# Fifty-eight gate and up chunks with the weights stationary and 256 tokens moving

## The chip, the core and the metric

The kernel runs on one core of one Trainium2 chip. The metric is the device time of one launch in microseconds (us), the median of three runs. PE is TensorE's matmul, PEld its weight load (the operand that stands in the array is loaded once for every matmul instruction), DVE is VectorE, ACT ScalarE, POOL GpSimd, SP SyncE.

## What is computed

Two blocks of two layers each over 256 tokens of width 1024, in float32. There are six feed-forward networks (FFN) of hidden width 2816, one after each mixer and in the first block one ahead of it too; the mixers (a short convolution, differential attention, retention, stick-breaking attention) are not touched by the change.

```python
def swiglu(x, w_gu, w_down):
    gate, up = jnp.split(x @ w_gu, 2, axis=-1)
    return (jax.nn.silu(gate) * up) @ w_down

h = h + 0.5 * rmsnorm(swiglu(rmsnorm(h, g[0]), ffn_w_gu[l, 0], ffn_w_down[l, 0]), g[1])
...
x = x + swiglu_2(rms_norm(x, ffn_norm[i]), ffn_w_in[i], ffn_w_out[i])
```

## The kernel before

The 256 tokens are two halves of 128. A product is kept exact to float32 by splitting each operand into a high and a low part of type fp32r and adding three products: high by high, high by low, low by high.

**Weights.** `plan` lists the weights as 279 units of 128 x 2048 numbers (1 MB each), in the order of use. `Weights.load` brings a unit to a `raw` tile, `split` makes `whi` on ACT (L162) and `wlo` on DVE (L163), each in two pieces of 128 x 1024 ahead of other work (`high_priority`). `pump` splits as long as one of five slots is free. On the host, `layout` orders the numbers of each row of 512 so that a read which takes columns 0, 256, 1, 257, ... (`columns`, "p (r a) -> p a r") gives the true order. Every weight moves in that alternating order.

**Tokens.** `T_gain` transposes a half of h and writes it with the norm's gain as `xT` (high and low): hidden index on the partitions, 128 tokens in a row. It is the operand that stands in PE. The norm's factor `rstd` is per token, that is per partition of the product, and is applied when the product is read.

**An FFN** (`ffn`) has 11 chunks of 256 hidden columns. For a chunk, `gu` runs for each half and each of two units four steps of `mm_col` with three matmuls (`mm3`, L259 to L261): tokens stand, 512 weight columns (256 gate, 256 up) move, and 128 tokens x 512 columns gather in one of two PSUM banks `mm`. Then ACT applies SiLU to the gate (L397), DVE multiplies with up (L399), which gives `hid`, tokens on partitions. The second product needs it the other way round, so `tr` transposes it on PE, two 128 x 128 blocks a half (L408, `tr_h`), and `split_plain` writes `hT` high (ACT, L310) and low (DVE, L311). `dn` then multiplies `hT` of two chunks earlier with a down unit into `acc` (`mm_row`, L282, L285, L288).

**Order.** A chunk in the steady state is 48 matmuls of `gu`, 24 of `dn` and 4 transposes. Four FFNs (f01, f11, f20, f21) have `skew`: their chunks 0 and 1 run by halves as `heads`, between the steps of the previous stage's end. f00 and f10 run all chunks in `body`. Engines run in the order that a scheduler gives at build time.

Of the kernel before, what the change touches and what calls it, by code (L numbers as in the profile page):

```python
# [11 lines left out]
F32 = mybir.dt.float32  # L12
F32R = mybir.dt.float32r
AF = mybir.ActivationFunctionType
ALU = mybir.AluOpType
# [3 lines left out]
P = 128  # L19
D = 1024  # L20
KD = D // P
FF = 2816
NCH = FF // 256
# [6 lines left out]
SLACK = 30  # L30
PIECES = 2


def plan():

    units = []

    def cols(key, w, idx, *segs):
        for j in range(2):
            units.append(((key, j), w, idx, 4 * j, segs))

    def row(key, j, w, idx):
        units.append(((key, j), w, idx, 2 * j, ((0, D),)))

    def ffn(tag, w_gu, w_dn, idx):  # L50
        for c in range(NCH):
            cols((tag, "gu", c), w_gu, idx, (c * 256, 256), (FF + c * 256, 256))
            if 2 <= c < NCH - 1:
                row((tag, "dn"), c - 2, w_dn, idx)
        for c in range(NCH - 3, NCH):
            row((tag, "dn"), c, w_dn, idx)

    def chunks(tag, w, which):
        for c in which:
            cols((tag, c), w, (0,), (c * 512, 512))  # L60

    def rows(tag, w, which):
        for j in which:
            row(tag, j, w, (0,))

    ffn("f00", "ffn_w_gu", "ffn_w_down", (0, 0))
    for c in range(4):
        cols(("cz", c), "conv_w_in", (0,), (D + c * 256, 256), (2 * D + c * 256, 256))
    chunks("cb", "conv_w_in", range(2))
    rows("co", "conv_w_out", range(4))  # L70
    ffn("f01", "ffn_w_gu", "ffn_w_down", (0, 1))
    for c in range(2):
        cols(("kv", c), "w_kv", (), (c * 512, 512))
    ffn("f10", "ffn_w_gu", "ffn_w_down", (1, 0))
    chunks("q", "attn_w_q", range(2))
    for c in range(2, 4):
        cols(("kv", c), "w_kv", (), (c * 512, 512))
    rows("ao", "attn_w_o", range(4))
    ffn("f11", "ffn_w_gu", "ffn_w_down", (1, 1))
    chunks("ri", "ret_w_in_2", range(11))  # L80
    rows("ro", "ret_w_o_2", range(2))
    chunks("ri", "ret_w_in_2", [11])
    rows("ro", "ret_w_o_2", range(2, 8))
    ffn("f20", "ffn_w_in_2", "ffn_w_out_2", (0,))
    chunks("si", "sb_w_in_2", [0, 1, 2, 4, 3, 5])
    rows("so", "sb_w_o_2", range(4))
    ffn("f21", "ffn_w_in_2", "ffn_w_out_2", (1,))
    return units


def layout(inputs):

    a = {name: np.asarray(v) for name, v in inputs.items()}
    units = plan()
    w = np.empty((len(units), P, 2048), np.float32)
    for i, (_, name, idx, k0, segs) in enumerate(units):
        nk = 2048 // sum(n for _, n in segs)
        rows = a[name][idx][k0 * P : (k0 + nk) * P].reshape(nk, P, -1).transpose(1, 0, 2)
        np.concatenate([rows[:, :, c : c + n] for c, n in segs], axis=2, out=w[i].reshape(P, nk, -1))
        w[i] = w[i].reshape(P, 4, 256, 2).transpose(0, 1, 3, 2).reshape(P, 2048)  # L100
    gains = [a["norm_g"], a["mix_norm_2"], a["ffn_norm_2"], a["ret_out_norm_2"], a["conv_k"], a["kv_norm_g"]]
    gains += [a["sb_q_norm_2"]] * 2 + [a["sb_k_norm_2"]] * 2 + [a["attn_subln_g"]]
    return {
        "x": a["x"],
        "x_t": np.ascontiguousarray(a["x"][0].reshape(2, P, KD, P).transpose(0, 3, 2, 1)),
        "w": w,
        "gains": np.ascontiguousarray(np.concatenate([g.ravel() for g in gains]).reshape(-1, P).T),
        "norm_g": a["norm_g"],
        "attn_lambda": a["attn_lambda"],
        **constants(),  # L110
    }
# [74 lines left out]
def tile_two_models(ctx: ExitStack, tc: tile.TileContext, a: dict):  # L186
# [6 lines left out]
    const = pool("const", 1)  # L193
    raw_pool = pool("raw", RAW)
    part_pool = pool("part", SLOTS)
    xt_pool = pool("xt", 1)
    k8 = pool("k8", 1)
    k4 = pool("k4", 4)
# [23 lines left out]
    gains = const.tile([P, NG], F32, tag="gains", name="gains")  # L222
    h = [const.tile([P, D], F32, tag=f"h{i}", name=f"h{i}") for i in range(2)]

    def g_cols(first, n):
        return gains[:, first : first + n]

# [20 lines left out]
    def new_mm():  # L248
        return ps_mm.tile([P, 512], F32, tag="mm", name="mm")

    def new_tr(name):
        return ps_tr.tile([P, 512], F32, tag="tr", name=name)
# [21 lines left out]
    def mm_row(acc, xT, kts, key, j, first, end, last):  # L274
# [14 lines left out]
        if last:  # L289
            W.done((key, j))  # L290

    def new_xT(half, place=None):
        if place is not None:
            t = big(place, [P, 2, KD, P], F32R, f"xk{half}")
        else:
            t = xt_pool.tile([P, 2, KD, P], F32R, tag=f"xT{half}", name=f"xT{half}")
        return t[:, 0], t[:, 1]

    def split_gain(tr, gcols, hi, lo):

# [8 lines left out]
    def split_plain(tr, hi, lo):  # L309
        S.copy(hi, tr)  # L310
        V.tensor_tensor(lo, tr, hi.bitcast(F32), ALU.subtract)  # L311
# [11 lines left out]
    def rms_of(half):  # L323
        ms, r = small(tag="ms"), small(tag=f"rstd{half}")
        S.activation(junk(D), h[half], AF.Square, scale=1 / 32, accum_out=ms)
        power(r, ms, EPS)
        return r


    def add_plain(half, acc):  # L330
# [54 lines left out]
    def ffn(tag, xT, rstd, skew=True, first=None, last_stage=False):  # L385
# [4 lines left out]
        def gu(c, half, j, last=True):  # L390
# [3 lines left out]
            if j == 1:  # L394
# [4 lines left out]
                V.scalar_tensor_tensor(t, ps[:, 256:512], rstd[half], sg, ALU.mult, ALU.mult)  # L399
                hid[c, half] = t  # L400

        def tr(c, half):
            if c not in hT:
                hT[c] = k4.tile([P, 2, 2, 2, P], F32R, tag="k4", name=f"hT{c}")
            t = new_tr("tr_h")
            src = hid.pop((c, half))
            for k in range(2):
                T.transpose(t[:, k * P : k * P + P], src[:, k * P : k * P + P], ident)  # L408
            split_plain(t[:, 0:256].rearrange("p (k t) -> p k t", k=2), hT[c][:, half, 0], hT[c][:, half, 1])
# [19 lines left out]

        def body():  # L430
            nonlocal first
            if not skew:
                for c in range(2):
                    for j in range(2):
                        for half in range(2):
                            gu(c, half, j, last=half == 1)
                            if first is not None:
                                first()
                                first = None
                        W.pump()  # L440
                    if c == 1:
                        for half in range(2):
                            tr(0, half)
            for c in range(2, NCH):
                for j in range(2):
                    for half in range(2):
                        gu(c, half, j, last=half == 1)
                        if c == 2 and j == 0:
                            tr(1, half)
                    W.pump()  # L450
                if c < NCH - 1:
                    for half in range(2):
                        dn(c - 2, half, last=half == 1)
                        tr(c, half)
                    W.pump()

        def tail_step(c, half):
            def run():
                dn(c, half, last=half == 1)
                if half == 0 and c == NCH - 3:  # L460
                    tr(NCH - 1, 0)
                if half == 0 and c == NCH - 2:
                    tr(NCH - 1, 1)

            return run

# [176 lines left out]
    def attention(xT, rstd, xk, rstd_k, kT):  # L643
# [67 lines left out]
        def s3(g, half):  # L711
            nh, n, s, sums = st.pop((g, half))
            sv = sums.rearrange("p (h c) -> p h c", c=2)
            if half not in r0s:
                r0s[half] = small(8, tag=f"r0{half}")
                if half == 0:
                    asb[half] = k4.tile([P, 8, n], F32, tag="k4", name="aA")
                else:
                    asb[half] = xt_pool.tile([P, 8, n], F32, tag="xT1", name="aB")
            hs = slice(g * nh, g * nh + nh)  # L720
            rec = small(8, tag="rec")[:, 0 : 2 * nh]
            V.reciprocal(rec, sums)
            rv = rec.rearrange("p (h c) -> p h c", c=2)
            cf = small(4, tag="cf")[:, 0:nh]
            V.scalar_tensor_tensor(cf, rv[:, :, 1], nlam, sv[:, :, 0], ALU.mult, ALU.mult)
            V.tensor_copy(r0s[half][:, hs], rv[:, :, 0])
            for i in range(nh):
                V.scalar_tensor_tensor(
                    asb[half][:, g * nh + i], s[:, i, 1], cf[:, i : i + 1], s[:, i, 0], ALU.mult, ALU.add
                )  # L730
# [290 lines left out]
    def stick(xT, rstd):  # L1021
# [56 lines left out]
        def l1(i):  # L1078
# [14 lines left out]
            if i < 6:  # L1093
                l, sp = (k4.tile([P, D], F32, tag="k4", name=n)[:, 0 : 6 * P] for n in ("l", "sp"))
            else:
                t = xt_pool.tile([P, 2, 6 * P], F32, tag=f"xT{i - 6}", name=f"l{i}")
                l, sp = t[:, 0], t[:, 1]
            l, sp = (t.rearrange("p (e t) -> p e t", e=2) for t in (l, sp))
            if i == 6:
# [269 lines left out]
```

## Time and profile before

| | us |
|---|---|
| median of 3 runs | 1613.62 (1613.02 to 1614.09) |
| the profiled execution | 1613.5 |
| its span on the core | 1611.7 |
| PE busy | 1580.7, 98% of the span |
| PEld busy (beside PE) | 1360.0, 84% |
| DVE busy | 968.6, 60% |
| ACT busy | 863.2, 54% |

Some 2 us lie around the span. The granted TensorE clock is 0.999 of full speed over the whole span, which is the level of 2.4 GHz. A matmul's busy time is its way through the array and overlaps the next one's; what a matmul costs in a stream is the distance from one start to the next, read from a timeline or from the chain that ended last.

### The profile page before, as it was taken

Reading aid. Unit: us, or ns where it says so; the run is one execution under the profiler, and the core shown is the slowest. Engines: PE = TensorE matmul, PEld = TensorE weight load, DVE = VectorE, ACT = ScalarE, POOL = GpSimd, SP = SyncE. Lnnn points to the kernel's source line nnn. Section 1 sums busy time; section 2 is a strip of 40 time slices with the busy share of each in tenths; the row PEclk is TensorE's granted clock in tenths of the full one; section 3 lists DMA queues with packets and bytes.
Section 4 is the critical chain, followed back from the end, with each engine's and each line's share of the span. In section 5 each row is a group of like instructions: output and inputs, shape, how many; then the busy total and the mean of one; then the engine's idle time right before and its main releaser. Section 6 shows DMA issues by size and latency. Waiting matters only on the chain.

```text
span 1611.7 us, 19563 instructions
## 1 busy us (share of the span) xinstructions
PE 1580.7 (98%) x7688; PEld 1360.0 (84%) x7688; DVE 968.6 (60%) x1385; ACT 863.2 (54%) x1385; POOL 61.2 (4%) x65
## 2 busy tenths in 40 slices
PE   7999999999999999999999999999999999999999
PEld 6888888888888888777888878888888888688887
DVE  6655767655565555688555676456555566665553
ACT  7544656444565444676444555456444476755442
POOL 0000000000000000101000010000000021000000
PEclk9999999999999999999999999999999999999999
DMA  8655645555545555444555645535455553235551
GB/s 322 243 206 187 244 157 176 204 205 187 209 173 203 188 205 193 147 176 145 183 206 188 239 175 183 183 141 205 175 192 205 189 207 134 103 135 207 207 189 46
DMA packets 42860, 300.79 MB, mean 187 GB/s; under 512 B 4800, under 2 KB 4928, under 8 KB 7312
## 3 DMA queue, kind: packets, MB, share of 16 engines
q1 hardware_dynamic: 42336, 297.91, 51.4%
q0 software_dynamic: 432, 1.64, 0.3%
q8 instruction: 60, 0.98, 0.2%
q14 instruction: 32, 0.26, 0.0%
HBM read 298.48 MB, written 1.05 MB: 186 GB/s over the span
## 4 chain that ended last, share of the span: by engine, by line
PE 87%; DVE 5%; ACT 4%; issue 1%; POOL 1%; DMA 1%; SPq 0%; ACTq 0%; POOLq 0%; DVEq 0%
PE mm L261 19%; PE mm L260 19%; PE mm L259 19%; PE acc L288 8%; PE acc L282 8%; PE acc L285 8%; PE tr_h L408 2%; DVE wlo L163 2%; PE tr L507 1%; ACT whi L162 1%; POOL r L346 1%; DVE h L348 1%; PE tr_x L319 1%; PE z L1119 1%; ACT s L706 1%
## 5 line engine op out<-in xcount | busy, mean ns | idle before, releaser
L163 DVE TENSOR_TENSOR wlo<-raw,whi 128x1024 fp32r<-128x1024 f32 x532 | 634.5, 1221 | 377.1 <-ACT whi L162 376.3
L162 ACT CAST whi<-raw 128x1024 fp32r<-128x1024 f32 x532 | 538.2, 1050 | 343.6 <-PE mm L261 213.9
L259 PE MATMUL mm<-whi,xT 128*128 128x512 f32 x1384 | 537.0, 388 | 8.3 <-ACT whi L162 8.2
L260 PE MATMUL mm<-wlo,xT 128*128 128x512 f32 x1384 | 525.9, 380 | 0.5 <-DVE wlo L163 0.5
L261 PE MATMUL mm<-whi,xT 128*128 128x512 f32 x1384 | 525.7, 380 | 0.7 <-DVE xT L304 0.7
L259 PEld LDWEIGHTS mm<-whi,xT 128*128 128x128 f32 x1384 | 262.2, 189 | 45.5 <-ACT whi L162 8.2
L261 PEld LDWEIGHTS mm<-whi,xT 128*128 128x128 f32 x1384 | 262.0, 189 | 39.0 <-DVE xT L304 1.7
L260 PEld LDWEIGHTS mm<-wlo,xT 128*128 128x128 f32 x1384 | 262.3, 190 | 36.3 <-DVE wlo L163 1.3
L282 PE MATMUL acc<-whi,hT 128*128 128x512 f32 x516 | 159.1, 390 | 0.4 <-ACT hT L310 0.4
L397 ACT ACTIVATE sg<-mm,rstd 128x256 f32<-128x256 f32 x132 | 62.7, 475 | 174.4 <-PE mm L261 174.3
L288 PE MATMUL acc<-whi,hT 128*128 128x512 f32 x516 | 153.8, 379 | 0.0
L285 PE MATMUL acc<-wlo,hT 128*128 128x512 f32 x516 | 153.5, 379 | 0.0
L399 DVE SCALAR_TENSOR_TENSOR hid<-mm,rstd,sg 128x256 f32<-128x256 f32 x132 | 63.4, 481 | 117.2 <-ACT sg L397 115.2
L285 PEld LDWEIGHTS acc<-wlo,hT 128*128 128x128 f32 x516 | 97.5, 189 | 13.8
L288 PEld LDWEIGHTS acc<-whi,hT 128*128 128x128 f32 x516 | 97.5, 189 | 13.8
L282 PEld LDWEIGHTS acc<-whi,hT 128*128 128x128 f32 x516 | 92.7, 189 | 11.0 <-ACT hT L310 0.6
L310 ACT CAST hT<-tr_h 128x256 fp32r<-128x256 f32 x132 | 49.2, 374 | 37.4 <-PE tr_h L408 37.4
L311 DVE TENSOR_TENSOR hT<-tr_h,hT 128x256 fp32r<-128x256 f32 x132 | 55.1, 418 | 6.4 <-ACT hT L310 6.4
L408 PE MATMUL tr_h<-ident,hid 128*128 128x128 f32 x264 | 50.2, 273 | 0.0
L408 PEld LDWEIGHTS tr_h<-ident,hid 128*128 128x128 f32 x264 | 37.2, 141 | 13.2
L304 DVE SCALAR_TENSOR_TENSOR xT<-tr_x,gains,xT 128x128 fp32r<-128x128 f32 x144 | 39.0, 344 | 15.3 <-ACT xT L302 15.3
L302 ACT ACTIVATE xT<-tr_x,gains 128x128 fp32r<-128x128 f32 x144 | 39.4, 391 | 13.2 <-PE tr_x L319 13.2
(222 smaller groups left out, 1239.9 us busy)
## 6 DMA issues: line engine op xcount, KB each, us to landing
raw<-in_w SPq DMA_DIRECT2D x277, 1024.0 KB, 4.8
gb<-in_norm_g SPq DMA_DIRECT2D x6, 512.0 KB, 5.6
raw<-in_w SPq DMA_DIRECT2D x2, 512.0 KB, 5.9
h<-in_x SPq DMA_DIRECT2D x2, 512.0 KB, 10.0
dec<-in_decay POOLq DMA_DIRECT2D x1, 768.0 KB, 6.4
x_t<-in_x_t SPq DMA_DIRECT2D x2, 256.0 KB, 4.1
x_t<-in_x_t SPq DMA_DIRECT2D x1, 512.0 KB, 7.2
out<-h SPq DMA_DIRECT2D x1, 512.0 KB, 2.6
```

The source lines that it names most:

```text
L162: self.nc.scalar.copy(hi[:, c], raw[:, c])
L163: self.nc.vector.tensor_tensor(lo[:, c], raw[:, c], hi[:, c].bitcast(F32), ALU.subtract)
L259: T.matmul(o, xh, wh, start=start, stop=False)
L260: T.matmul(o, xh, wl, start=False, stop=False)
L261: T.matmul(o, xl, wh, start=False, stop=stop)
L282: T.matmul(acc[:, n * 512 : n * 512 + 512], xh(kts + k), columns(wh, c), start=st, stop=False)
L285: T.matmul(acc[:, n * 512 : n * 512 + 512], xh(kts + k), columns(wl, c), start=False, stop=False)
L288: T.matmul(acc[:, n * 512 : n * 512 + 512], xl(kts + k), columns(wh, c), start=False, stop=sp[n])
L311: V.tensor_tensor(lo, tr, hi.bitcast(F32), ALU.subtract)
L397: S.activation(sg, ps[:, 0:256], AF.Silu, scale=rstd[half])
L399: V.scalar_tensor_tensor(t, ps[:, 256:512], rstd[half], sg, ALU.mult, ALU.mult)
L408: T.transpose(t[:, k * P : k * P + P], src[:, k * P : k * P + P], ident)
```

## The change

For 58 of the 66 chunks (all eleven of f00 and f10, chunks 2 to 10 of the others) the operands change places. 128 gate or up columns of the weights stand, and 256 tokens of both halves move; the product has hidden columns on its partitions, so nothing is transposed. `xT` becomes one tile for both halves, in which the tokens of a step are 256 neighbouring numbers: they move in plain order, and the weights of these chunks are no longer reordered on the host. Since `rstd` now varies along the row, `across` makes a tile `rows` that holds it for all partitions, with two matmuls an FFN, and `gated` multiplies gate and up by it before SiLU. The tiles of attention and stick-breaking that shared `xT`'s memory share the new tile.

```diff
     def ffn(tag, w_gu, w_dn, idx):
         for c in range(NCH):
-            cols((tag, "gu", c), w_gu, idx, (c * 256, 256), (FF + c * 256, 256))
+            moving = tag not in WHOLE and c < 2
+            cols((tag, "gu", c), w_gu, idx, (c * 256, 256), (FF + c * 256, 256), moving=moving)
...
+        if half == 0:
+            xts.append(xt_pool.tile([P, 2, KD, 2, P], F32R, tag="xT", name="xT"))
+        return xts[-1][:, 0, :, half], xts[-1][:, 1, :, half]
...
+    def across(rstd):
+        t = new_tr("tr_r")
+        for half in range(2):
+            d = wk.tile([P, 256], F32, tag="hid", name="spread")[:, 0:P]
+            V.tensor_copy(d, rstd[half].broadcast_to([P, P]))
+            T.matmul(t[:, half * P : half * P + P], d, ident, start=True, stop=True)
+        S.copy(rows, t[:, 0 : 2 * P])
...
+        def whole(c, j):
+            wh, wl = W.get(((tag, "gu", c), j))
+            for b in range(2):
+                if j == 0:
+                    gu_ps[c, b] = new_mm()
+                ps = gu_ps[c, b]
+                for k in range(4):
+                    kk = 4 * j + k
+                    xh, xl = (xts[-1][:, i, kk].rearrange("p r a -> p (r a)") for i in range(2))
+                    for n in range(2):
+                        w = slice(k * 512 + n * 256 + b * P, k * 512 + n * 256 + b * P + P)
+                        o = ps[:, n * 256 : n * 256 + 256]
+                        for m, (st, mv) in enumerate(((wh, xh), (wh, xl), (wl, xh))):
+                            T.matmul(
+                                o, st[:, w], mv, start=kk == 0 and n == 0 and m == 0, stop=kk == 7 and m == 2,
+                                skip_group_check=True,
+                            )
+                if j == 1:
+                    gated(c, b)
+            W.done(((tag, "gu", c), j))
+
+        def gated(c, b):
...
+            for n in range(2):
+                V.tensor_tensor(t[:, n], ps[:, n], r, ALU.mult)
...
+            S.activation(sg, t[:, 0], AF.Silu)
...
+            V.tensor_tensor(hd, t[:, 1], sg, ALU.mult)
+            split_plain(hd, hT[c][:, :, 0, b], hT[c][:, :, 1, b])
...
-            for c in range(2, NCH):
+            for c in range(2 if skew else 0, NCH):
                 for j in range(2):
-                    for half in range(2):
-                        gu(c, half, j, last=half == 1)
-                        if c == 2 and j == 0:
+                    whole(c, j)
...
+                    if skew and c == 2 and j == 0:
+                        for half in range(2):
                             tr(1, half)
+                    if c == (2 if skew else 0) and j == 0:
+                        across(rstd)
```

On PE, in f00 between two chunks, the kernel before has this at the end of a `gu` (L261), through `dn` for both halves, to the next `gu` (L259):

```order
L261 MATMUL mm<-whi_960,xT_145 128x512
L282 MATMUL acc_455<-whi_994,hT_937 128x512 x2
...
L288 MATMUL acc_455<-whi_994,hT_937 128x512 x2
L408 MATMUL tr_h<-ident,hid 128x128 x2
L282 MATMUL acc_474<-whi_994,hT_937 128x512 x2
...
L288 MATMUL acc_474<-whi_994,hT_937 128x512 x2
L408 MATMUL tr_h<-ident,hid 128x128 x2
L259 MATMUL mm<-whi_1034,xT_120 128x512
```

The changed kernel at the same place (L435 is the matmul of `whole`; L288, L291, L294 are those of `dn`):

```order
L291 MATMUL acc_631<-wlo_1033,hT_899 128x512 x2
L294 MATMUL acc_631<-whi_1032,hT_899 128x512 x2
L435 MATMUL mm<-xT,whi_1107 128x256 x2
L435 MATMUL mm<-xT,wlo_1108 128x256
L435 MATMUL mm<-xT,whi_1107 128x256 x2
L435 MATMUL mm<-xT,wlo_1108 128x256
```

The transposes are gone, and one `gu` matmul of 512 columns has become two of 256, 96 a chunk. In the whole program L435 stands 5568 times, the transposes of `tr` fall from 264 to 32, and 12 matmuls of `across` are added.

DVE in f00, one chunk, before (L399 gives `hid` of each half, L311 the low part of `hT`, L163 splits weights):

```order
L399 SCALAR_TENSOR_TENSOR hid<-mm,rstd_171,sg 128x256
L399 SCALAR_TENSOR_TENSOR hid<-mm,rstd_178,sg 128x256
L163 TENSOR_TENSOR wlo_1035<-raw_923,whi_1034 128x1024 x2
L311 TENSOR_TENSOR hT_1054<-tr_h,hT_1054 128x256
L163 TENSOR_TENSOR wlo_1078<-raw_966,whi_1077 128x1024
L311 TENSOR_TENSOR hT_1054<-tr_h,hT_1054 128x256
```

And in the changed kernel (L451 and L455 are in `gated`, L321 is the low part of `hT`, L167 splits weights):

```order
L451 TENSOR_TENSOR gated<-mm,rows 128x256 x2
L167 TENSOR_TENSOR wlo_1108<-raw_948,whi_1107 128x1024
L455 TENSOR_TENSOR hid<-gated,sg 128x256
L167 TENSOR_TENSOR wlo_1108<-raw_948,whi_1107 128x1024
L321 TENSOR_TENSOR hT_1064<-hid,hT_1064 128x2x128
```

For each of a chunk's two banks DVE now has four instructions of 128 x 256 where it had two, and the two that read the bank stand first.

## Rows read from the trace of the kernel before

**Rows 1.** The page's busy times: us, share of the span, instructions.
```profile
PE 1580.7 (98%) x7688; PEld 1360.0 (84%) x7688; DVE 968.6 (60%) x1385; ACT 863.2 (54%) x1385; POOL 61.2 (4%) x65
```

**Rows 2.** The chain that ended last, one chunk of f00: start, us, what.
```profile
91.39 0.43 PE acc L282 x2
...
93.98 0.22 PE tr_h L408 x2
...
96.79 0.22 PE tr_h L408 x2
97.01 0.22 PE mm L259
...
107.37 0.43 PE acc L282 x2
```

**Rows 3.** Two stretches of f00: us, busy PE, PEld, DVE, ACT, POOL; clock, DMA, GB/s.
```profile
91.00:123.00 32.00, 32.00 (x154) 27.94 (x153) 17.25 (x20) 14.93 (x20) 0.00 (x0) 1.00 0.54 197
```

**Rows 4.** One line's instructions: xcount, duration ns min/median/max, first and last start.
```profile
L260 PE MATMUL mm<-wlo,xT x1384: 379/379/796, 9.5 to 1591.3; 128*128 128x512 f32 x198
L1119 PE MATMUL z<-sp,later x24: 486/486/590, 1356.1 to 1398.6; 128*128 128x384 f32 x24
L1088 PE MATMUL z<-sbr x14: 332/340/440, 1348.4 to 1403.5; 128*128 128x384 f32 x14
L1088 PE MATMUL mm<-sbr x2: 423/431/439, 1393.2 to 1396.1; 128*128 128x384 f32 x2
```

**Rows 5.** The chain that ended last, around L1088, L1119 and L1120 of stick-breaking.
```profile
1352.72 0.35 PE z L1088 x2
...
1383.23 0.22 PE z L1120 x2
1383.45 0.35 PE z L1088 x2
...
1396.39 0.18 PE mm L1088
```

**Rows 6.** The page's groups: line, engine, what, xcount; busy us, mean ns; idle before.
```profile
L163 DVE TENSOR_TENSOR wlo<-raw,whi 128x1024 fp32r<-128x1024 f32 x532 | 634.5, 1221 | 377.1 <-ACT whi L162 376.3
L399 DVE SCALAR_TENSOR_TENSOR hid<-mm,rstd,sg 128x256 f32<-128x256 f32 x132 | 63.4, 481 | 117.2 <-ACT sg L397 115.2
L311 DVE TENSOR_TENSOR hT<-tr_h,hT 128x256 fp32r<-128x256 f32 x132 | 55.1, 418 | 6.4 <-ACT hT L310 6.4
```

**Rows 7.** The timeline of the start: start us, us, engine, line, what, idle before.
```profile
8.21 0.80 PE L259 MATMUL mm<-whi,xT 128*128 128x512 f32 x1 [8.21 <-ACT whi L162]
9.46 0.80 PE L260 MATMUL mm<-wlo,xT 128*128 128x512 f32 x1 [0.46 <-DVE wlo L163]
...
10.31 2.46 ACT L302 ACTIVATE xT<-x_t,gains 128x128 fp32r<-128x128 f32 x8
...
11.51 2.18 DVE L304 SCALAR_TENSOR_TENSOR xT<-x_t,gains,xT 128x128 fp32r<-128x128 f32 x8
```

More of the change, by code (lines that the diff above doesn't have):

```diff
@@ L31, with cols @@
 PIECES = 2
+WHOLE = "f00", "f10"
 def plan():
     units = []
-    def cols(key, w, idx, *segs):
+    def cols(key, w, idx, *segs, moving=True):
         for j in range(2):
-            units.append(((key, j), w, idx, 4 * j, segs))
+            units.append(((key, j), w, idx, 4 * j, segs, moving))
     def row(key, j, w, idx):
-        units.append(((key, j), w, idx, 2 * j, ((0, D),)))
+        units.append(((key, j), w, idx, 2 * j, ((0, D),), True))
     def ffn(tag, w_gu, w_dn, idx):
         for c in range(NCH):
-            cols((tag, "gu", c), w_gu, idx, (c * 256, 256), (FF + c * 256, 256))
+            moving = tag not in WHOLE and c < 2
+            cols((tag, "gu", c), w_gu, idx, (c * 256, 256), (FF + c * 256, 256), moving=moving)
             if 2 <= c < NCH - 1:
@@ L95, in layout @@
     w = np.empty((len(units), P, 2048), np.float32)
-    for i, (_, name, idx, k0, segs) in enumerate(units):
+    for i, (_, name, idx, k0, segs, moving) in enumerate(units):
         nk = 2048 // sum(n for _, n in segs)
@@ L99, in layout @@
         np.concatenate([rows[:, :, c : c + n] for c, n in segs], axis=2, out=w[i].reshape(P, nk, -1))
-        w[i] = w[i].reshape(P, 4, 256, 2).transpose(0, 1, 3, 2).reshape(P, 2048)
+        if moving:
+            w[i] = w[i].reshape(P, 4, 256, 2).transpose(0, 1, 3, 2).reshape(P, 2048)
     gains = [a["norm_g"], a["mix_norm_2"], a["ffn_norm_2"], a["ret_out_norm_2"], a["conv_k"], a["kv_norm_g"]]
@@ L223, in tile_two_models @@
     h = [const.tile([P, D], F32, tag=f"h{i}", name=f"h{i}") for i in range(2)]
+    rows = const.tile([P, 2 * P], F32, tag="rows", name="rows")
     def g_cols(first, n):
@@ L290, in mm_row @@
             W.done((key, j))
+    xts = []
     def new_xT(half, place=None):
@@ L294, in new_xT @@
             t = big(place, [P, 2, KD, P], F32R, f"xk{half}")
-        else:
-            t = xt_pool.tile([P, 2, KD, P], F32R, tag=f"xT{half}", name=f"xT{half}")
-        return t[:, 0], t[:, 1]
+            return t[:, 0], t[:, 1]
+        if half == 0:
+            xts.append(xt_pool.tile([P, 2, KD, 2, P], F32R, tag="xT", name="xT"))
+        return xts[-1][:, 0, :, half], xts[-1][:, 1, :, half]
     def split_gain(tr, gcols, hi, lo):
@@ L400, in gu @@
                 hid[c, half] = t
+        def whole(c, j):
[19 more added lines that the diff above has]
+        def gated(c, b):
+            if c not in hT:
+                hT[c] = k4.tile([P, 2, 2, 2, P], F32R, tag="k4", name=f"hT{c}")
+            ps = gu_ps.pop((c, b)).rearrange("p (n r a) -> p n r a", n=2, r=2)
+            t = k2.tile([P, 2, 2, P], F32, tag="k2", name="gated")
+            r = rows.rearrange("p (r a) -> p r a", r=2)
+            for n in range(2):
+                V.tensor_tensor(t[:, n], ps[:, n], r, ALU.mult)
+            sg = wk.tile([P, 256], F32, tag="sg", name="sg").rearrange("p (r a) -> p r a", r=2)
+            S.activation(sg, t[:, 0], AF.Silu)
+            hd = wk.tile([P, 256], F32, tag="hid", name="hid").rearrange("p (r a) -> p r a", r=2)
+            V.tensor_tensor(hd, t[:, 1], sg, ALU.mult)
+            split_plain(hd, hT[c][:, :, 0, b], hT[c][:, :, 1, b])
         def tr(c, half):
@@ L431, in body @@
             nonlocal first
-            if not skew:
-                for c in range(2):
-                    for j in range(2):
-                        for half in range(2):
-                            gu(c, half, j, last=half == 1)
[L437 to L441, printed above, removed]
-                        for half in range(2):
-                            tr(0, half)
-            for c in range(2, NCH):
-                for j in range(2):
-                    for half in range(2):
-                        gu(c, half, j, last=half == 1)
-                        if c == 2 and j == 0:
+            for c in range(2 if skew else 0, NCH):
+                for j in range(2):
+                    whole(c, j)
+                    if first is not None:
+                        first()
+                        first = None
+                    if skew and c == 2 and j == 0:
+                        for half in range(2):
                             tr(1, half)
+                    if c == (2 if skew else 0) and j == 0:
+                        across(rstd)
                     W.pump()
-                if c < NCH - 1:
+                if 2 <= c < NCH - 1:
                     for half in range(2):
                         dn(c - 2, half, last=half == 1)
-                        tr(c, half)
                     W.pump()
@@ L459, in run @@
                 dn(c, half, last=half == 1)
[L460 to L463, printed above, removed]
             return run
@@ L718, in s3 @@
                 else:
-                    asb[half] = xt_pool.tile([P, 8, n], F32, tag="xT1", name="aB")
+                    asb[half] = xt_pool.tile([P, 8, n], F32, tag="xT", name="aB")
             hs = slice(g * nh, g * nh + nh)
@@ L1095, in l1 @@
             else:
-                t = xt_pool.tile([P, 2, 6 * P], F32, tag=f"xT{i - 6}", name=f"l{i}")
+                if i == 6:
+                    st["last"] = xt_pool.tile([P, 2, 2, 6 * P], F32, tag="xT", name="l67")
+                t = st["last"][:, i - 6]
                 l, sp = t[:, 0], t[:, 1]
```

## The prediction

> **What bounds the kernel now.** I read the busy times first: PE is busy for 98% of the span, DVE for 60%, ACT for 54% [rows 1]. Busy PE is not proof, since matmuls overlap in the trace, so I went to the chain that ended last. Inside an FFN it holds PE alone: the first `dn` matmuls of two chunks that follow each other stand at 91.39 and 107.37, which is 15.98 us [rows 2]. That is 72 matmuls of 512 columns and 4 transposes. A pair of transposes takes 0.22 [rows 2], so one takes 0.11 and four 0.44, and (15.98 - 0.44) / 72 = 0.2158 us for a matmul. At 2.4 GHz, the granted clock of these stretches [rows 3], 512 columns at one a cycle are 0.2133. So the stream loses 2.5 ns an instruction and otherwise nothing: no wait on a weight, a bank or another engine. DVE is busy for 17.25 and ACT for 14.93 of 32 us there [rows 3]. Every nanosecond put on PE in an FFN chunk, or taken from it, moves the end. The question is therefore only what 96 matmuls of 256 plain columns cost against 48 of 512 alternating ones.
>
> **The change, part by part.**
>
> *Removed from PE.* 232 transposes (264 less 32) at 0.11 us [rows 2]: 25.5 us, all on the path. Also 58 x 48 = 2784 matmuls at 0.2158: 600.8 us. A changed chunk's gate and up work thus costs 48 x 0.2158 + 0.44 = 10.80 us today.
>
> *Added to PE.* 58 x 96 = 5568 matmuls of 256 columns, as many columns in all as before. Each costs p, which no row shows. Four facts bound it.
>
> First, the floor. 256 columns at one a cycle are 106.7 ns, and 2.5 ns go to the instruction: 109.2 ns.
>
> Second, plain order. The alternating read takes 379 ns from start to end for 512 columns [rows 4]; less 213.3 of columns this leaves 166 ns of way. L1119 is a float32 matmul in plain order at two cycles a column: 486 ns for 384 columns, which is 166 + 320, no loss [rows 4]. The one fp32r matmul in plain order is L1088, also 384 columns. Without loss it would take 166 + 160 = 326 ns; it takes 332 at least and 340 in the median [rows 4]. The chain says the same in another way: two take 0.35 us, one 0.18 [rows 5], so some 0.175 each where 160 + 2.5 = 162.5 ns would do. Plain order at one column a cycle loses 6 to 17 ns on 384 columns, typically 12.5. The whole gain of the alternating order is that it loses nothing.
>
> Third, how that loss scales. If with the columns, 256 lose two thirds: at least 4 ns (from 332), typically 8.3 (from 0.175), at most 11.7 (from 0.18), so p is 113 to 121 ns. If it falls once on each instruction, it is 12.5 to 17.5, and p is 121.7 to 126.7. I take the columns, since what the rows show is a rate that a longer read would pay again: p = 118 ns, which is 109.2 and the typical 8.3, rounded.
>
> Fourth, the load. Twice as many loads must hide behind half as long a matmul. L1088's second group, which had nothing to hide behind, took 423 to 439 ns against 340 [rows 4], so a bare load costs 83 to 99 ns. L1120, a pass of 128 columns at two cycles (107 ns of stream, as long as the new matmul), has a load each and takes 0.22 for two [rows 5]. So the load fits under 107 ns, by a small margin, and is priced at nothing. If that cover fails, it would cost what it exceeds, 5 ns or so on each matmul, 28 us; that is within the case of the fixed loss.
>
> The rows show that alternate reads 1 KB apart run at full rate and neighbours do not. The Trainium skill, SBUF — State Buffer, "Door 1", says the reverse, that accesses within the same 16-byte line run at full bandwidth and each crossing to a new line pays. By it plain order would cost 109.2 ns; the measured 0.2158 for alternating columns contradicts it, and the measurement decides.
>
> So 5568 x 0.118 = 657.0 us. Against 600.8 this is +56.2, and with the transposes gone +30.7, or 11.33 against 10.80 us for a chunk. The break-even is 10.80 / 96 = 112.5 ns.
>
> *`across`.* 12 passes of 128 columns at 0.11 [rows 5]: +1.3 us. Its DVE and ACT work lies beside 48 matmuls.
>
> *The start.* Today the first matmul runs at 8.21, as soon as half 0 and the first weights are there [rows 7]. Now it needs half 1 as well: its first high part comes at the start of the ACT row at 10.31 plus an eighth of 2.46, so 10.6, its low part on DVE at 11.8 [rows 7]. The loss is 2.4 to 3.6 us; I take 3.
>
> *DVE and ACT.* For each bank DVE has four instructions instead of two. At 0.48 each at most (L399, L311 [rows 6]) a chunk adds 4 x 0.48 = 1.9 us to some 8.6 of 15.98 [rows 3], so DVE stays at about 63%. What it hands on is the PSUM bank. After the last matmul of a bank, 24 matmuls of the other bank and 24 of `dn` follow, 24 x 0.118 + 24 x 0.2158 = 8.0 us. DVE needs two reads of 0.48 and may have two weight pieces of 1.22 ahead of them [rows 6]: 3.4. Hidden. Only in chunks 0 to 2 of f00 and f10 is there no `dn` yet, and the cover is 2.8: four hand-overs, 0 to 1.5 us each; I take 2 us in all. Where DVE's reads are late, the split of the next weights queues behind them on DVE, with slots ahead of use.
>
> *The shared `xT` tile.* It now waits for the readers of both halves of what was there. Those readers are PE instructions ahead in PE's own queue, so this is nothing.
>
> **Sum.** +30.7 + 1.3 + 3 + 2 = +37.0. The profiled execution took 1613.5, which is the median of the runs within 0.1; forecast **1651 us**, 2.3% slower.
>
> **Rivals.**
>
> *Plain order costs nothing here* (ends on the other side). Place: each L435. L1088 reads both its operands from one tile `sbr`; here the weights stand in one tile and the tokens move from another. If the loss came from that sharing, p is 109.2, a chunk costs 10.48, and 58 x (10.80 - 10.48) = 18.6 is gained, less 6.3: 1601 us. Against it: L1088 is also over 326 ns in its lowest row, with the way of its load no different from L260's. For it: there is only one such operation in the trace, 16 times. It decides as soon as p is under 111.4 ns, where 58 chunks give back the 6.3. The Trainium skill, TensorE: Matmul & The Clock Gate, "Back-to-back issue gap", gives 262 cycles for 256 columns whatever their order, which is this case; the 512 alternating columns agree with its 518 cycles (0.2158).
>
> *The loss is paid by the instruction, or the load no longer hides.* p is 121.7 to 126.7, middle 124: a chunk costs 11.90, and 58 x 1.10 + 6.3 = +70: 1684 us. For it: a load runs beside nearly all of each matmul, where it ran beside half. Against it: L1120 shows a load under 107 ns.
>
> *The bank comes late in every chunk.* For it: two banks, and SiLU now stands behind a DVE product. Against it: 8.0 us of cover against 3.4, and SiLU reads SBUF, so it doesn't hold the bank. At 0.5 us a chunk it would add 29: 1680. It needs DVE to be 5 us behind; little chance.
>
> **How the numbers follow.** Loss with the columns (p 113 to 121, 1623 to 1668, likeliest 1651): 0.55. Paid by the instruction, or load not hidden: 0.15. Late banks: 0.03. No loss: 0.23. About break-even (1610 to 1617): 0.04. A measurement of this kernel can tell some 0.2% from no change. So faster 0.23, same 0.04, slower 0.73. The range reaches down to the likeliest time of the no-loss case, 1600, and up to 1682, the lower half of the fixed loss; about 0.11 lies below and 0.08 above.
>
> **What would show it.** In the trace after, the distance of starts of L435 inside a chunk: 118 ns is my case, 109 the first rival, 122 to 127 the second. The `dn` of two chunks that follow should stand 96 x 0.118 + 24 x 0.2158 = 16.5 us apart, not 15.98; 15.7 in the first rival. No gap on PE before the first L435 of a chunk; one there with DVE's L451 as its releaser would be the third rival. The first matmul at 10.6 and not 8.21. The 32 transposes left must be those of chunks 0 and 1. What would break the forecast most is p, on which 5568 instructions rest: a nanosecond is 5.6 us.

## The result

The changed kernel takes 1658.83 us (median, 1658.12 to 1659.42) against 1613.66 before (the three runs of the table above and a fourth): a ratio of 1.0281 (95% interval 1.0268 to 1.0294), 45.2 us slower. The forecast was 1651, slower, range 1600 to 1682. The spans of the two profiled executions differ by 1657.5 - 1611.7 = 45.8 us.

The page of the changed kernel, busy times first (us, share of the span, instructions; [rows 1] answers to them), then the two groups of the new matmul and the one of DVE's reads of its bank:

```profile
PE 1625.6 (98%) x10264; PEld 1485.9 (90%) x10264; DVE 1050.5 (63%) x1629; ACT 867.0 (52%) x1391; POOL 61.1 (4%) x65
...
L435 PE MATMUL mm<-xT,whi 128*128 128x256 f32 x3712 | 674.2, 284 | 11.5 <-ACT xT L312 11.3
...
L435 PE MATMUL mm<-xT,wlo 128*128 128x256 f32 x1856 | 525.6, 283 | 0.0
...
L451 DVE TENSOR_TENSOR gated<-mm,rows 128x256 f32<-128x256 f32 x232 | 87.2, 417 | 20.0 <-PE mm L435 19.7
```

PE is as full as before, with 2576 instructions more. Before the 5568 new matmuls PE stood idle for 11.5 us in all, and 11.3 of that is the start of the program. DVE waits for PE, not the other way round.

The chain that ended last, one chunk of f00 (start, us, what; [rows 2] answers to it):

```profile
98.75 0.43 PE acc L288 x2
...
103.94 11.51 PE mm L435 x96
115.45 0.43 PE acc L288 x2
```

A chunk takes 115.45 - 98.75 = 16.70 us, 0.72 more than the 15.98 before. 96 matmuls of 256 columns take 11.51, 120 ns each, with nothing between them. The timeline has the same distance, start to start:

```profile
109.76 0.28 PE L435 MATMUL mm<-xT,wlo 128*128 128x256 f32 x1
109.88 0.40 PE L435 MATMUL mm<-xT,whi 128*128 128x256 f32 x2
110.12 0.28 PE L435 MATMUL mm<-xT,wlo 128*128 128x256 f32 x1
110.24 0.40 PE L435 MATMUL mm<-xT,whi 128*128 128x256 f32 x2
110.48 0.28 PE L435 MATMUL mm<-xT,wlo 128*128 128x256 f32 x1
```

Three matmuls in 0.36 us. The stretch of the chunk (us; busy PE, PEld, DVE, ACT, POOL; clock, DMA, GB/s; [rows 3] answers to it):

```profile
98.75:115.46 16.71, 16.71 (x122) 16.07 (x121) 10.02 (x14) 7.54 (x11) 0.00 (x0) 1.00 0.54 187
```

The clock is the full 2.4 GHz as before, DVE is at 10.02 / 16.71 = 60%, and the load, PEld, is now busy for 96% of the time, where it was 27.94 of 32 [rows 3].

### The profile page after: what moved, and what is told of

Read it like the earlier page. It is cut to its first block, busy times and chain, and to the rows that moved or that the text cites. A ratio compares the mean times of both kernels' runs of the same rounds, so it can differ in the third digit from the quotient of the medians.

```text
span 1657.5 us, 25235 instructions
## 1 busy us (share of the span) xinstructions
PE 1625.6 (98%) x10264; PEld 1485.9 (90%) x10264; DVE 1050.5 (63%) x1629; ACT 867.0 (52%) x1391; POOL 61.1 (4%) x65
## 4 chain that ended last, share of the span: by engine, by line
PE 88%; DVE 5%; ACT 4%; POOL 1%; issue 1%; DMA 0%; SPq 0%; ACTq 0%; POOLq 0%
PE mm L435 40%; PE acc L294 8%; PE acc L288 8%; PE acc L291 8%; PE mm L267 7%; PE mm L265 6%; PE mm L266 6%; DVE wlo L167 1%; PE tr L551 1%; ACT whi L166 1%; POOL r L365 1%; PE tr_x L329 1%; DVE h L367 1%; PE z L1165 1%; ACT s L750 1%
## 5 line engine op out<-in xcount | busy, mean ns | idle before, releaser
L167 DVE TENSOR_TENSOR wlo<-raw,whi 128x1024 fp32r<-128x1024 f32 x532 | 635.1, 1221 | 385.3 <-ACT whi L166 384.3
L435 PE MATMUL mm<-xT,whi 128*128 128x256 f32 x3712 | 674.2, 284 | 11.5 <-ACT xT L312 11.3
L435 PEld LDWEIGHTS mm<-xT,whi 128*128 128x128 f32 x3712 | 583.3, 192 | 14.4 <-ACT xT L312 11.3
L435 PE MATMUL mm<-xT,wlo 128*128 128x256 f32 x1856 | 525.6, 283 | 0.0
L435 PEld LDWEIGHTS mm<-xT,wlo 128*128 128x128 f32 x1856 | 356.4, 192 | 0.0
L265 PE MATMUL mm<-whi,xT 128*128 128x512 f32 x456 | 178.9, 392 | 0.1
L267 PE MATMUL mm<-whi,xT 128*128 128x512 f32 x456 | 173.3, 380 | 0.8 <-DVE xT L314 0.8
L266 PE MATMUL mm<-wlo,xT 128*128 128x512 f32 x456 | 173.2, 380 | 0.0
L288 PE MATMUL acc<-whi,hT 128*128 128x512 f32 x516 | 153.9, 380 | 0.0
L294 PE MATMUL acc<-whi,hT 128*128 128x512 f32 x516 | 153.9, 380 | 0.0
L291 PE MATMUL acc<-wlo,hT 128*128 128x512 f32 x516 | 153.5, 379 | 0.0
L294 PEld LDWEIGHTS acc<-whi,hT 128*128 128x128 f32 x516 | 97.5, 189 | 14.1 <-DVE hT L321 0.3
L291 PEld LDWEIGHTS acc<-wlo,hT 128*128 128x128 f32 x516 | 97.4, 189 | 13.9
L288 PEld LDWEIGHTS acc<-whi,hT 128*128 128x128 f32 x516 | 93.7, 190 | 10.7
L451 DVE TENSOR_TENSOR gated<-mm,rows 128x256 f32<-128x256 f32 x232 | 87.2, 417 | 20.0 <-PE mm L435 19.7
L265 PEld LDWEIGHTS mm<-whi,xT 128*128 128x128 f32 x456 | 86.2, 189 | 14.1 <-issue 2.3
L267 PEld LDWEIGHTS mm<-whi,xT 128*128 128x128 f32 x456 | 86.2, 189 | 14.0 <-DVE xT L314 1.7
L266 PEld LDWEIGHTS mm<-wlo,xT 128*128 128x128 f32 x456 | 86.3, 189 | 11.8 <-issue 1.0
L321 DVE TENSOR_TENSOR hT<-hid,hT 128x256 fp32r<-128x256 f32 x116 | 48.8, 420 | 24.6 <-ACT hT L320 24.6
```

What stands on the lines that cost most here:

```text
L167: self.nc.vector.tensor_tensor(lo[:, c], raw[:, c], hi[:, c].bitcast(F32), ALU.subtract)
L265: T.matmul(o, xh, wh, start=start, stop=False)
L266: T.matmul(o, xh, wl, start=False, stop=False)
L267: T.matmul(o, xl, wh, start=False, stop=stop)
L288: T.matmul(acc[:, n * 512 : n * 512 + 512], xh(kts + k), columns(wh, c), start=st, stop=False)
L291: T.matmul(acc[:, n * 512 : n * 512 + 512], xh(kts + k), columns(wl, c), start=False, stop=False)
```

## The experiments

At 120 ns a matmul loses 10.8 on the 109.2 that its columns need. Three theories: **A**, plain order loses with the columns, as the prediction took it; **B**, plain order loses once an instruction; **C**, twice as many loads no longer hide, and the order has little to do with it.

**Tokens in alternating order.** The changed kernel, with the two halves moving in turn:

```diff
-                    xh, xl = (xts[-1][:, i, kk].rearrange("p r a -> p (r a)") for i in range(2))
+                    xh, xl = (xts[-1][:, i, kk].rearrange("p r a -> p a r") for i in range(2))
...
-            ps = gu_ps.pop((c, b)).rearrange("p (n r a) -> p n r a", n=2, r=2)
+            ps = gu_ps.pop((c, b)).rearrange("p (n a r) -> p n r a", n=2, r=2)
```

> The changed kernel, in which the 256 tokens of a gate and up matmul move alternately, one of half 0 and one of half 1 (neighbours in time are 512 bytes apart), and the product is read in that order. Theory A, the loss belongs to plain order and the load of the weights hides: a matmul falls from 120.1 to 109.2 ns, 5568 of them give back 61 us, so about 1598 us, 1% below the kernel before. Theory B, the loss is paid once an instruction because of plain order: the same 1598. Theory C, twice as many loads don't hide and the load sets 120 ns whatever the order: 1659 as the changed kernel, no gain.

Measured: 1614.93 us, ratio to the kernel before 1.0007 (0.9997 to 1.0017). This is between the theories: 43.9 us, 7.9 ns a matmul, belong to the order, but 109.2 was not reached. The chain that ended last, one chunk:

```profile
101.01 10.72 PE mm L435 x96
111.72 0.43 PE acc L288 x2
```

10.72 / 96 = 111.7 ns. Something other than the stream stops it 2.5 ns short; the load is the candidate.

**128 tokens a matmul.** The changed kernel with each matmul in two, so that the stream is far shorter than a load:

```diff
-                            T.matmul(
-                                o, st[:, w], mv, start=kk == 0 and n == 0 and m == 0, stop=kk == 7 and m == 2,
+                            for r in range(2):
+                                T.matmul(
+                                    o[:, r * P : r * P + P], st[:, w], mv[:, r * P : r * P + P],
...
```

> The changed kernel with each gate and up matmul cut into two of 128 tokens, so 11136 of them, each with its own load; the stream of one is 128 plain columns, 61 ns by theory A, so the load must be the bound and shows what it takes beside a matmul. Theories A and B, a load takes 107 to 109 ns: 11136 x 0.109 - 669 = +545, about 2204 us. Theory C, a load takes 120 ns beside a matmul: +668, about 2327 us. Well under 107 ns would show that a load is far from being a bound at 256 columns.

Measured: 2317.7 us, in a single run. By the total this is close to theory C's 2327, but the total holds more than the load. The chain that ended last, in f00, a first stretch and one chunk later:

```profile
59.87 75.73 PE mm L436 x355
135.61 0.96 PE acc L288 x2
...
139.40 0.43 PE acc L288 x2
...
168.61 21.39 PE mm L436 x192
```

Up to some 138 us the new matmuls stand 213 ns apart, and a pair of `dn`, which moves the old way, takes 0.96 where it takes 0.43 later: PE ran at half its pace there. Two later stretches of this run have the same pace, and there the windows give the granted clock as half, the level of 1.2 GHz (us; busy PE, PEld, DVE, ACT, POOL; clock, DMA, GB/s):

```profile
1185.00:1205.00 20.00, 20.00 (x93) 19.46 (x92) 4.65 (x10) 3.68 (x7) 0.00 (x0) 0.52 0.16 52
1663.00:1683.00 20.00, 20.00 (x92) 19.46 (x91) 4.61 (x10) 3.64 (x7) 0.00 (x0) 0.51 0.15 53
```

PE had stood idle for 1.2 us shortly before each of the two. For the first stretch the windows print 1.00, but the trace holds no entry of the clock before some 138 us, where the full pace begins. So the lower clock is the likely reason there too, though no entry shows it. Some 730 of the new matmuls went at half pace, and that is some 75 us of the total. A chunk at full pace shows the load itself: 21.39 / 192 = 111.4 ns. The total bears it out: 11136 x 0.1114 - 668 = 572 us more than the changed kernel, and the 75, make 2306 of the 2317.7. So a load beside matmuls takes 111.4 ns. It is the bound of the run before (111.7), and it is under the 120 of the changed kernel, where the plain stream decides. Theory C falls as the cause of the 120, and a smaller part of it stands: with loads of 111.4 a matmul can't come down to 109.2, however well the tokens are ordered. That it is the load which sets this distance, and not the issue of the instructions, is shown by the loads that read apart, below: only their reading changes, and the distance with it. The transposes, a load and a matmul each, also cost less, 0.108 (below).

**Plain order at 512 columns.** The kernel before with its weights moving as they lie (and not reordered on the host):

```diff
-        return w[:, first : first + 512].rearrange("p (r a) -> p a r", r=2)
+        return w[:, first : first + 512]
```

> The kernel before, with its 6672 moving weight reads of 512 columns in plain order and the weights not reordered on the host; nothing else. Theory A, the loss goes with the columns: 256 columns lose 120.1 - 109.2 = 10.9 ns, 512 lose 21.8, a matmul takes 237.6 ns instead of 215.8, and the whole 1614 + 145 = 1759 us. Theory B, the loss is paid once an instruction: 226.7 ns and 1614 + 73 = 1687 us. Theory C, the load is the bound at 256 columns and plain order costs little: 216 to 218 ns and 1614 to 1630 us.

Measured: 1686.04 us, ratio 1.0447 (1.0426 to 1.0467): 72.1 us on 6672 matmuls, 10.8 ns each. The chain that ended last, at a pair of `dn` matmuls, which took 0.43 [rows 2]:

```profile
113.02 0.45 PE acc L284 x2
113.48 0.45 PE acc L287 x2
```

This is theory B, which gave 1687. 512 columns lose 10.8 ns, 256 lose 10.8 as well: the loss is paid once an instruction. Theory A would have had 1759. Each instruction here has one load of 128 columns, so a loss paid once a load would look the same.

**No transposes.** The kernel before, with `hid` split as it is; this leaves the transposes of the FFNs out, so the second products take a block that isn't transposed.

```diff
-            t = new_tr("tr_h")
             src = hid.pop((c, half))
-            for k in range(2):
-                T.transpose(t[:, k * P : k * P + P], src[:, k * P : k * P + P], ident)
-            split_plain(t[:, 0:256].rearrange("p (k t) -> p k t", k=2), hT[c][:, half, 0], hT[c][:, half, 1])
+            split_plain(src.rearrange("p (k t) -> p k t", k=2), hT[c][:, half, 0], hT[c][:, half, 1])
```

> The kernel before without the 264 transposes of hid on PE: ACT and DVE split hid as it is, so the second product of each FFN is of a block that isn't transposed. It prices the part of the change that saves. By the step of the prediction, 0.11 us each and all on the path: 29 us less, 1585 us. Rival, PE waits elsewhere for what the transposes covered: 1595 to 1610 us.

Measured: 1585.50 us, ratio 0.9824 (0.9804 to 0.9843): 28.5 us for 264, 0.108 each. The saving of the change is real and all on the path; it is only smaller than what replaces it.

**Loads that read apart.** If alternating helps the stream, does reading apart help the load? The stationary operand takes one step only, so the weights were stored for a step of four numbers (16 bytes), with alternating tokens and, second, with plain ones:

```diff
+        if not moving:
+            w[i] = w[i].reshape(P, 4, 4, 128).transpose(0, 1, 3, 2).reshape(P, 2048)
...
-                        w = slice(k * 512 + n * 256 + b * P, k * 512 + n * 256 + b * P + P)
+                        w = slice(k * 512 + 2 * n + b, k * 512 + 512, 4)
```

> The run with alternating tokens, in which the weights that stand are stored so that the load takes every fourth number (16 bytes apart) instead of 128 neighbours. The run of 128 tokens showed 111 ns from load to load with hardly a stream to hide behind, the one with alternating tokens 112 ns where the stream needs 109.2. Theory L, the load in plain order loses as the stream does, and apart it takes at most 109: 109.2 ns, 5568 x 2.8 = 16 us below the run with alternating tokens, 1599 us. Rival M, the load takes 111 to 112 ns however it reads: 1615 us, no change. Rival N, reading apart makes the load slower: over 1620 us.

> The changed kernel (256 tokens in plain order) with the same loads of every fourth number. Theory B1, the 11 ns a matmul are lost by the plain stream itself, whatever the load beside it does: 120 ns, 1659 us. Theory B2, they are lost because load and stream read in the same manner at the same time: 112 ns or less, 1615 us or less.

Measured: 2283.02 us (ratio 1.4148, 1.4126 to 1.4169) and 2284.40 (1.4157, 1.4131 to 1.4183). Rival N, and far beyond its 1620: a chunk's 96 matmuls now take 22.30 us in the chain that ended last, 232 ns each and twice the 111.7. One line's instructions in the first (duration in ns, min/median/max):

```profile
L437 PEld LDWEIGHTS mm<-xT,whi x3712: 307/330/336, 11.2 to 2260.4; 128*128 128x128 f32 x196
```

330 ns against 192 for neighbours (below, under what was not expected). With a load this long the second of the two runs can't show the stream at all; it tells nothing on B1 and B2. Whether the load beside it has a part in the 10.8 ns stays open.

**Alternating within 16 bytes' reach.** Tokens in the order 0, 4, 1, 5, 2, 6, 3, 7, 8, 12, ...:

```diff
-                    xh, xl = (xts[-1][:, i, kk].rearrange("p r a -> p (r a)") for i in range(2))
+                    xh, xl = (xts[-1][:, i, kk].rearrange("p r a -> p (r a)").rearrange("p (c r e) -> p c e r", r=2, e=4) for i in range(2))
...
```

> The changed kernel with tokens moving alternately within one half: 0, 4, 1, 5, 2, 6, 3, 7, then 8, 12, ..., that is between neighbouring groups of 16 bytes and not between places 512 bytes apart. Which part of plain order costs 11 ns a matmul: if it is enough that neighbours in time don't lie in the same 16 bytes, a matmul takes 112 ns (the load's bound) and the kernel 1615 us, as with 512 bytes. If the two must be further apart, 120 ns and 1659 us.

Measured: 1615.42 us, ratio 1.0014 (1.0004 to 1.0024), and a chunk is the same as with 512 bytes between:

```profile
99.88 10.72 PE mm L435 x96
110.60 0.43 PE acc L288 x2
```

So it is enough that two reads that follow each other are 16 bytes apart, in neighbouring groups of 16 bytes. It gives back at least 8.3 of the 10.8 ns (120.0 to 111.7); the load hides whether the last 2.5 went too. Whether the groups of 16 bytes count, or only that the two numbers are not neighbours, no run shows: an order such as 0, 2, 1, 3 was not run.

**Fewer loads.** The bound of 256 columns is now known: 120 plain, 111.7 alternating. High and low tokens move under one load of the high weights, as 512 alternating columns; the low weights take 256. The two parts of the product gather in separate columns, in four banks, and are added on the way out. `xb` is the tile of the step with both parts, halves alternating; the bank for `across` and the place of chunk 1's transposes are moved to make room.

```diff
-                        for m, (st, mv) in enumerate(((wh, xh), (wh, xl), (wl, xh))):
...
+                        o = gu_ps[c, b][n]
+                        T.matmul(o, wh[:, w], xb, start=kk == 0, stop=False, skip_group_check=True)
+                        T.matmul(o[:, 0:256], wl[:, w], xb[:, 0], start=False, stop=kk == 7, skip_group_check=True)
...
+                lo = wk.tile([P, 256], F32, tag="sg", name="lo")
+                S.copy(lo, pss[n][:, 256:512])
+                V.tensor_tensor(lo, pss[n][:, 0:256], lo, ALU.add)
```

> Alternating tokens, and the high and low parts of the tokens move as one matmul of 512 columns under one load of the high weights (their two products gather in separate columns, in four banks, and ACT and DVE add them); the low weights take 256 columns as before. Per three products two loads instead of three. If the load of 111 to 112 ns is the bound of a 256-column matmul: 215.8 + 112 = 327.8 ns for what took 3 x 112 = 336 with alternating tokens and 3 x 120.1 = 360 in the changed kernel; 1856 x 32.5 ns = 60 us below the changed kernel, 1599 us plus up to 6 us where a bank comes late or the transposes of chunk 1 are waited for: 1599 to 1605, 0.6 to 0.9% below the kernel before. Rival, the added work makes DVE (some 12 of 15.7 us a chunk) or the banks the bound: 1620 us or more.

Measured: 1607.73 us, ratio 0.9964 (0.9952 to 0.9977): 5.9 us faster than the kernel before, though not the 9 to 15 expected. The matmuls do what they should (timeline, start us, us, ...):

```profile
100.03 0.27 PE L434 MATMUL mm<-xT,wlo 128*128 128x256 f32 x1
100.14 0.38 PE L433 MATMUL mm<-xT,whi 128*128 128x512 f32 x1
100.36 0.27 PE L434 MATMUL mm<-xT,wlo 128*128 128x256 f32 x1
100.47 0.38 PE L433 MATMUL mm<-xT,whi 128*128 128x512 f32 x1
```

A pair takes 0.327 us, what 215.8 + 111.4 gives. The rest went elsewhere: to the start (the next run), to PE's waits for `h` where a stage begins (`tr_x`, 8.2 us where the kernel before has 6.0), and, 2.3 us in all, to the end of four FFNs, where the longer way from the last bank to `hT` is no longer covered and ends on PE (chain that ended last, f00; start, us, what):

```profile
177.77 0.43 DVE gated L450
...
179.25 0.42 DVE hid L454
...
179.69 0.41 ACT hT L320
...
180.15 0.70 PE acc L288 x2
```

**The start by halves.** The same, with chunks 0 and 1 of f00 in the old form:

```diff
-            moving = tag not in WHOLE and c < 2
+            moving = tag != "f10" and c < 2
...
+            if tag == "f00":
+                for c in range(2):
+                    for j in range(2):
+                        for half in range(2):
+                            gu(c, half, j, last=half == 1)
+                        W.pump()
...
```

> The run with high and low tokens in one matmul, in which chunks 0 and 1 of f00, the first of the program, keep the old form (tokens stand, one half at a time, with transposes). It tests the start term: the first matmul again at 8.2 us instead of 12.3. If the start is the loss it looks like (the first weights come late whichever operand stands, so that 3 to 4 us are lost), 1607.7 falls by 3 to 4 and loses two chunks' gain of 0.3 each: about 1604 us. Rival, the weights of the next units set the start anyway: 1608 us.

Measured: 1605.13 us, ratio 0.9944 (0.9931 to 0.9958), 2.6 us below the run before it; the first matmul stands at 8.80:

```profile
8.80 0.79 PE L265 MATMUL mm<-whi,xT 128*128 128x512 f32 x1 [8.80 <-ACT whi L166]
```

With the 0.6 us that two chunks give up, waiting for both halves at the start cost some 3 us. The five runs spread from 1601.25 to 1605.83 and the two ratios' intervals overlap, so the 2.6 is uncertain; that the first matmul stands 3.5 us earlier than the 12.26 of the run before is not. This version is 0.6% faster than the kernel before.

## Why the prediction was right, and where it was off

**PE bounds every chunk: right.** The forecast said that each nanosecond put on PE there moves the end; 0.72 us a chunk, 58 times, is 41.8 of the 45.8 us.

**The price of a matmul: right in kind, 2 ns short.** That plain order loses on fp32r was read from one operation, 16 matmuls of L1088 [rows 4, 5], and it held for 5568. The step that failed is "how that loss scales": I took it to go with the columns, since a rate would be paid again by a longer read. Sizes 256 and 512 now show 10.8 ns each, and the 6 to 17 ns of the 384 columns of L1088 lie around it (162.5 + 10.8 is 0.347 us for two, which the chain prints as 0.35). It is paid once an instruction. That the forecast came as near as it did is partly luck: the 12.5 taken from L1088 is more than the 10.8 measured, two thirds of it are less, and the two errors partly cancel. By the distance alone 120 ns would even have spoken for the wrong case, since it lies in the range given to the columns (113 to 121) and below the one given to the instruction (121.7 to 126.7); only the run with 512 columns told them apart. The term is 5568 x 0.120 = 668 us and not 657, which is 11 of missing time.

**The load: priced at nothing, rightly, for a wrong reason.** L1120's 0.22 us for two passes [rows 5] was read as a load under 107 ns. At two decimals it stands for anything from 107.5 to 112.5 each, so it could not tell a load that fits from one that doesn't. A load of the new kind takes 111.4. It hides only because the plain stream takes 120. So the first rival, faster at 1601 with 109.2 ns, was out of reach with the weights stored as they are: in the two alternating orders that were run the kernel stands at 1615, level with before. The Trainium skill, TensorE: Matmul & The Clock Gate, "LDWEIGHTS (loading the stationary operand)", has columns / 1.2, 107 ns for 128; the run of 128 tokens measured 111.4 from load to load.

**The transposes: right.** 0.108 us each by the run without them; 232 are 25.1, forecast 25.5.

**`across`: 2.6, forecast 1.3.** Its 12 matmuls are in float32 and stand in the trace as 24 passes, four an FFN (L345, in f00 two pairs of 0.22 us in the chain that ended last). The forecast counted 12.

**The start: 2.5, forecast 3.** The first matmul stands at 11.33 and not at 10.6. The changed kernel's first matmuls and the first at the full distance:

```profile
11.33 0.80 PE L435 MATMUL mm<-xT,whi 128*128 128x256 f32 x2 [11.33 <-ACT xT L312]
12.32 0.58 PE L435 MATMUL mm<-xT,whi 128*128 128x256 f32 x1 [0.19 <-DVE xT L314]
...
15.45 0.40 PE L435 MATMUL mm<-xT,whi 128*128 128x256 f32 x2
```

By its timeline it has then done 16 matmuls, worth 16 x 0.120 = 1.9 us, as if it had begun at 13.5. The kernel before reaches its full distance here, after 9 matmuls, worth 1.9 as well, as if it had begun at 11.0:

```profile
12.97 0.38 PE L259 MATMUL mm<-whi,xT 128*128 128x512 f32 x1
```

**The banks: 0, forecast 2.** No L435 but the first ones had idle time before it. The third rival falls with that. The sum: 5568 x 0.120 - 600.8 = 67.4, so 67.4 + 2.6 + 2.5 - 25.1 = 47.4 of the 45.8 us measured. The rest is a term that the forecast didn't have: PE's idle time, start apart, fell from 22.3 us (1611.7 - 1580.7, less 8.7) to 20.4 (1657.5 - 1625.6, less 11.5), which takes 1.9 off and leaves 45.5. No run tells why it fell.

## What to carry to other kernels

To swap which operand stands is to change how many columns move under one load; count columns, loads and the order in which the moving operand is read, each for itself, before counting what is saved beside them. Where matmuls stream back to back, price each from the distance of starts: here 2 ns a matmul were 11 us. A loss that one size shows may belong to the instruction or to the column, and a second size in the same trace, or a run with one thing changed, tells which.

## What was not expected of the hardware

- Plain order of the moving fp32r operand costs 10.8 ns an instruction, at 256 and at 512 columns alike; alternating between two neighbouring groups of 16 bytes removes all of it that the load lets one see. Why it is paid once, and whether the load beside it matters, no run here shows.
- The load goes the other way. Neighbours take 111.4 ns for 128 columns, numbers 16 bytes apart 232: with alternating tokens the step added 2283.0 - 1614.9 = 668 us to 5568 loads, 120 ns on each, over the 111.7. The load's rows of the run with alternating tokens, to set beside the 330 above:

```profile
L435 PEld LDWEIGHTS mm<-xT,whi x3712: 186/192/338, 11.7 to 1594.0; 128*128 128x128 f32 x196
```

The Trainium skill, SBUF — State Buffer, "Door 1", says that reads within one 16-byte line run at full rate and that each crossing pays. The load agrees with it (192 against 330 ns). The moving operand does not: crossing at every read cost nothing that shows, and reading the four numbers of each line in turn cost 10.8 ns an instruction.
- 96% busy loads [the stretch above] are no sign that loads bound a stream: the changed kernel's matmuls stood 120 ns apart beside them, where the load alone would have let them stand at 111.4.
